# Seven instead of six pairs of each down projection as seven block products, with a second home for the summed weights

## The chip, the cores and the metric

One core of a Trainium2 chip runs the whole program. The metric is the device time of one execution in microseconds (us), the median of repeated runs. The profile is of one execution; its engines are called PE (TensorE, the matmuls), DVE (VectorE), ACT (ScalarE), POOL (GpSimd) and SP (the queue that issues the weight transfers).

## The reference, cut to what matters

A trunk of two layers on 256 positions of width 1024. Each layer adds half a SwiGLU block, a mixer, and half a SwiGLU block again, so there are four SwiGLU blocks, each with an inner width of 2816:

```
def swiglu(x, w_gate, w_up, w_down):
    return (jax.nn.silu(x @ w_gate) * (x @ w_up)) @ w_down

h = h + 0.5 * swiglu(rms_norm(h, ffn1_norm[layer]), ...)
h = h + mixer(rms_norm(h, mix_norm[layer]))
h = h + 0.5 * swiglu(rms_norm(h, ffn2_norm[layer]), ...)
```

The part that matters here is the last product, `(256 x 2816) @ (2816 x 1024)`, called the down projection.

## The kernel before

**Precision.** Every fp32 operand of a product is split in a high part (ACT copies it to fp32r) and a low part (DVE subtracts the high part from it), and a product is three matmuls: high by high, high by low, low by high (`mm3`). So each chunk of weights costs one pass on ACT and one on DVE before PE can use it.

**The stream of weights.** The class `Stream` moves all weights through the core in chunks of 128 x 2048 elements (1 MB), in one order for the whole program. `load_one` fetches a chunk into one of three `raw` buffers; `split_one` makes its parts in one of four `whi`/`wlo` buffers; `pump` does as much of both as the buffers allow, and runs whenever PE's program takes a chunk or gives one back. Instructions are put into each engine's queue at build time; an engine runs its queue in that order and waits where an input isn't ready or a buffer isn't free.

**The down projection.** The 22 tiles of the inner width (128 each) are taken as eleven pairs, named by their first tile, in the order of `DOWN`. The left operand is `hT`, two blocks of 128 positions (t = 0, 1); the right one is two halves of 512 columns (h = 0, 1). For one pair that is a 2 x 2 by 2 x 2 product of blocks: eight block products, 24 matmuls. For the pairs in `MIXED` the kernel computes it with seven block products of sums and differences of blocks, 21 matmuls (`mixed_part`). The sums of the left blocks are made when the inner tile is computed (`mix_rows`: four small DVE operations, one split into `seh`/`sel`). The sums of the weights are made in `split_mixed`: four DVE operations of 128 x 512 into `wx` (one of them changes `raw` in place), then ACT and DVE split `wx` into `wxh` and `wxl` (128 x 1536 each). Of the seven products four need the chunk's own parts (`own`) and three need the sums' parts (`sums`).

**Where the sums' parts lie.** `wxh` and `wxl` have one buffer each. The next mixed pair can write them only when PE has finished the `sums` products of the pair before. To ease that, every second pair does `sums` first and the others `own` first, and `split_mixed` makes its parts in the matching order (`lead`).

**After the products.** `project` ends with the last two pairs of `DOWN` for t = 0 (the residual `x0`, both halves), then for t = 1. The residual adds (`L269`, `L433` and the helper sums `L437`, `L438`), squares (ACT, `L278`), the mean (DVE, `L283`), the root (POOL, `L249`), the scaled copy `xn` (ACT, `L320`), PE's transposes (`L342`) and the split into `xTh`/`xTl` (`L352` on ACT, `L354` on DVE) lead to the first matmuls of the next block (`L381` to `L383`). `xTh`/`xTl` hold the turned x of the current block; the gate and up products (`colwise`, `L391` to `L393`) read them, and nothing reads them during a down projection.

Of the kernel before, what the change touches and what calls it, by code (L numbers as in the profile page):

```python
# [10 lines left out]
F32 = mybir.dt.float32  # L11
# [18 lines left out]
HEAT = 9  # L30
DOWN = [4, 6, 8, 0, 10, 12, 2, 14, 16, 18, 20]
MIXED = (6, 8, 10, 12, 14, 16)

# [5 lines left out]
class Stream:  # L39


    def __init__(self, nc, pools):
        self.nc, (self.raw_pool, self.hi_pool, self.lo_pool) = nc, pools
        self.specs, self.raws, self.parts = [], {}, {}
        self.loaded = self.split = self.done = self.next = self.mixes = 0

    def add(self, src, nk, w, shift=0, pieces=2, mixed=False):
# [48 lines left out]
    def split_mixed(self, j, raw, hi, lo):  # L96
        nc = self.nc
        lead = self.mixes % 2 == 0
        self.mixes += 1
        b11, b12, b21, b22 = (raw[:, i * 512 : (i + 1) * 512] for i in range(4))  # L100
        wx = self.mix_pool.tile([128, 3, 512], F32, name="wx")
        wxh, wxl = (self.mix_pool.tile([128, 3, 512], F32R, name=m) for m in ("wxh", "wxl"))
        nc.vector.tensor_sub(wx[:, 0, :], b22, b12)
        if not lead:
            self.split_piece(hi[:, 1024:], lo[:, 1024:], raw[:, 1024:])
        nc.vector.tensor_sub(b12, b12, b11)
        nc.vector.tensor_add(wx[:, 1, :], wx[:, 0, :], b11)
        nc.vector.tensor_sub(wx[:, 2, :], b21, wx[:, 1, :])  # L108
        if lead:
            self.split_piece(wxh, wxl, wx)  # L110
            self.split_piece(hi[:, 1024:], lo[:, 1024:], raw[:, 1024:])
        self.split_piece(hi[:, :1024], lo[:, :1024], raw[:, :1024])
        if not lead:
            self.split_piece(wxh, wxl, wx)
        self.parts[j] += (wxh, wxl)

    def pump(self):
        n = len(self.specs)
        while True:
            if self.loaded < n and self.loaded - RAW < self.split:  # L120
                self.load_one()
            elif self.split < self.loaded and self.split - SPL < self.done:
                self.split_one()
            else:
                break
# [24 lines left out]
def trunk(ctx: ExitStack, tc: tile.TileContext, a, out):  # L150
# [250 lines left out]
    def project(tiles, order, nfinal, factor, nxt, after=None, mixed={}):  # L401
# [10 lines left out]
        def mixed_part(k, w):  # L412
# [4 lines left out]
            x = [[v[:, j, :] for v in w[2:]] for j in range(3)]  # L417
            own = [((0, 0), a[1][0], b[1][0]), ((0, 1), e[2], b[1][1]), (1, a[0][0], b[0][0]), (5, e[0], b[0][1])]
            sums = [(7, a[0][1], x[0]), (6, e[1], x[1]), ((1, 0), a[1][1], x[2])]
            for key, s, m in sums + own if i % 2 == 0 else own + sums:  # L420
                single = type(key) is int
                if key not in banks:
                    banks[key] = bank()
                first = i == 0 if single else started(*key)
                mm3(banks[key], *s, *m, first, single and i == len(mixed) - 1)
# [232 lines left out]
    def ffn(phase, begin=None):  # L658
        with ExitStack() as pools:
# [55 lines left out]
            def mix_rows(k, hm):  # L715
# [5 lines left out]
                nc.vector.tensor_sub(e[:, 2, :], a12, e[:, 1, :])  # L721
                mixed[k] = [mq.tile([128, 3, 128], F32R, name=f"{n}{k}") for n in ("seh", "sel")]
                split(*mixed[k], e)
# [7 lines left out]
            else:  # L731
# [3 lines left out]
                finish(1)  # L735
            mq = st.mix_pool = pools.enter_context(tc.tile_pool(name="mq", bufs=1))
            mixed = {}
            for k in range(6 if begin else 2, FT, 2):
# [14 lines left out]

            turn_all()
            project(hT, [k + j for k in DOWN for j in range(2)], 4, 0.5, phase + 1, mixed=mixed)

# [319 lines left out]
```

## Time and profile before

| what | value |
|---|---|
| median of 3 runs | 925.23 us (924.93 to 925.3) |
| time of the profiled execution | 924.85 us |
| its span, first to last instruction | 923.1 us |
| PE busy | 915.7 us, 99% |
| DVE busy | 691.9 us, 75% |
| ACT busy | 538.2 us, 58% |

The profiled execution took 1.75 us more than its span, and 0.38 us less than the median. "Busy" is the time in which an engine runs an instruction; the durations of matmuls overlap, so what a matmul costs is read from one start to the next. The four down projections start at 126.92, 395.63, 573.62 and 860.71 us of the span.

### The profile page before, as it was taken

What the parts mean: (1) busy time and instruction counts of PE and PEld (TensorE: products, weight loads), DVE (VectorE), ACT (ScalarE), POOL (GpSimd) and SP (SyncE); (2) the same over time, 40 slices, a digit from 0 to 9 for tenths busy, and PEclk for the clock granted to TensorE, in tenths of its full rate; (3) what the DMA queues carried; (4) which work ended last, traced back from release to release, by engine and by line L of the source; (5) the groups of instructions that cost most, each with busy time, mean ns of one, the idle gap of its engine ahead of it and who ended that gap; (6) DMA issues with size and microseconds to landing.
All of it is one profiled execution on the core that took longest, in us unless ns stands there. A gap on an engine that the chain in (4) does not pass through costs nothing.

```text
span 923.1 us, 15780 instructions
## 1 busy us (share of the span) xinstructions
PE 915.7 (99%) x6442; PEld 843.2 (91%) x6442; DVE 691.9 (75%) x1044; ACT 538.2 (58%) x842; POOL 35.5 (4%) x53
## 2 busy tenths in 40 slices
PE   9999999999999999999999999999999999999997
PEld 8999998889889999988899999888989799999886
DVE  6886779977657566879876678898656575677797
ACT  6754555585867455546664555556756674555552
POOL 0000000000000000000000000000323100000000
PEclk9999999999999999999999999999999999999999
DMA  9885554757526766536486665473744457665351
GB/s 324 270 275 182 186 180 141 270 175 249 167 91 191 221 185 195 192 131 242 153 274 185 195 207 179 162 243 129 250 150 146 129 167 225 203 204 185 137 182 45
DMA packets 125704, 175.79 MB, mean 190 GB/s; under 512 B 3264, under 2 KB 104768, under 8 KB 125632
## 3 DMA queue, kind: packets, MB, share of 16 engines
q1 hardware_dynamic: 123952, 172.60, 57.5%
q10 hardware_dynamic: 1680, 2.19, 0.8%
q8 instruction: 50, 0.82, 0.4%
q14 instruction: 22, 0.18, 0.1%
HBM read 173.73 MB, written 1.05 MB: 189 GB/s over the span
## 4 chain that ended last, share of the span: by engine, by line
PE 99%; issue 1%; DVE 0%; ACT 0%; POOLq 0%; POOL 0%
PE bank L391 18%; PE bank L393 18%; PE bank L392 18%; PE bank L458 5%; PE bank L462 5%; PE bank L459 5%; PE bank L239 4%; PE bank L237 4%; PE bank L238 4%; PE bank L381 3%; PE bank L383 3%; PE bank L382 3%; PE bank L822 1%; PE bank L782 1%; PE bank L342 1%; PE bank L810 1%
## 5 line engine op out<-in xcount | busy, mean ns | idle before, releaser
L93 ACT ACTIVATE whi<-raw 128x1024 fp32r<-128x1024 f32 (+1 forms) x336 | 329.0, 1029 | 238.8 <-PE bank L392 102.8
L94 DVE TENSOR_TENSOR wlo<-raw,whi 128x1024 fp32r<-128x1024 f32 (+1 forms) x336 | 385.1, 1184 | 84.3 <-ACT whi L93 83.7
L391 PE MATMUL bank<-xTh,whi 128*128 128x256 f32 x1440 | 399.7, 278 | 0.0
L393 PE MATMUL bank<-xTh,wlo 128*128 128x256 f32 x1440 | 398.2, 277 | 0.0
L392 PE MATMUL bank<-xTl,whi 128*128 128x256 f32 x1440 | 398.2, 276 | 0.0
L391 PEld LDWEIGHTS bank<-xTh,whi 128*128 128x128 f32 x1440 | 270.3, 188 | 1.3 <-issue 1.2
L392 PEld LDWEIGHTS bank<-xTl,whi 128*128 128x128 f32 x1440 | 270.8, 188 | 0.1
L393 PEld LDWEIGHTS bank<-xTh,wlo 128*128 128x128 f32 x1440 | 270.5, 188 | 0.0
L674 DVE TENSOR_TENSOR hm<-sil,bank 128x512 f32<-128x512 f32 x38 | 26.1, 687 | 57.2 <-PE bank L393 57.1
L458 PE MATMUL bank<-whi,hTh 128*128 128x512 f32 x152 | 59.8, 393 | 0.0
L459 PE MATMUL bank<-wlo,hTh 128*128 128x512 f32 x152 | 59.2, 390 | 0.0
L242 ACT ACTIVATE hTh<-hm 128x512 fp32r<-128x512 f32 x39 | 24.5, 627 | 50.1 <-DVE hm L719 38.9
L462 PE MATMUL bank<-whi,hTl 128*128 128x512 f32 x152 | 51.4, 389 | 0.0
L94 DVE TENSOR_TENSOR wxl<-wx,wxh 128x1536 fp32r<-128x1536 f32 x24 | 42.1, 1755 | 11.3 <-ACT wxh L93 11.2
L381 PE MATMUL bank<-whi,xTh 128*128 128x512 f32 x112 | 44.4, 397 | 0.0
L383 PE MATMUL bank<-whi,xTl 128*128 128x512 f32 x112 | 43.8, 391 | 0.0
L382 PE MATMUL bank<-wlo,xTh 128*128 128x512 f32 x112 | 43.6, 390 | 0.0
L93 ACT ACTIVATE wxh<-wx 128x1536 fp32r<-128x1536 f32 x24 | 35.5, 1481 | 11.6 <-DVE wx L108 7.7
L249 POOL TENSOR_TENSOR rstd<-ms,half_neg 128x1 f32<-128x1 f32 x14 | 8.1, 582 | 797.2 <-DVE ms L283 792.9
L462 PEld LDWEIGHTS bank<-whi,hTl 128*128 128x128 f32 x152 | 28.5, 188 | 6.0
L459 PEld LDWEIGHTS bank<-wlo,hTh 128*128 128x128 f32 x152 | 28.6, 188 | 5.6
L458 PEld LDWEIGHTS bank<-whi,hTh 128*128 128x128 f32 x152 | 28.6, 188 | 5.5
(165 smaller groups left out, 1150.5 us busy)
## 6 DMA issues: line engine op xcount, KB each, us to landing
raw<-in_ffn_w_down SPq DMA_DIRECT2D x44, 1024.0 KB, 5.0
raw<-in_ffn_w_gate SPq DMA_DIRECT2D x38, 1024.0 KB, 5.5
raw<-in_ffn_w_up SPq DMA_DIRECT2D x38, 1024.0 KB, 5.4
raw<-in_c_w_in SPq DMA_DIRECT2D x12, 1024.0 KB, 5.4
raw<-in_ab_w_in SPq DMA_DIRECT2D x10, 1024.0 KB, 5.4
raw<-in_ffn_w_up SPq DMA_DIRECT2D x12, 512.0 KB, 6.5
raw<-in_ffn_w_gate SPq DMA_DIRECT2D x8, 512.0 KB, 4.0
raw<-in_ab_w_out SPq DMA_DIRECT2D x4, 1024.0 KB, 5.0
```

What stands on the lines that cost most here:

```text
L93: self.nc.scalar.activation(hi, raw, AF.Copy)
L94: self.nc.vector.tensor_sub(lo, raw, hi.bitcast(F32))
L237: nc.tensor.matmul(p, sh, mh, start=start, stop=False)
L381: nc.tensor.matmul(p, xh, w[0][:, k, :], start=k0 + k == 0, stop=False)
L382: nc.tensor.matmul(p, xh, w[1][:, k, :], start=False, stop=False)
L383: nc.tensor.matmul(p, xl, w[0][:, k, :], start=False, stop=k0 + k == KD - 1)
L391: nc.tensor.matmul(p, h, xh, start=k == 0, stop=False)
L392: nc.tensor.matmul(p, h, xl, start=False, stop=False)
L393: nc.tensor.matmul(p, l, xh, start=False, stop=k == KD - 1)
L458: nc.tensor.matmul(banks[t, h], sh, w[0][:, kw, cs], start=first, stop=False)
L459: nc.tensor.matmul(banks[t, h], sh, w[1][:, kw, cs], start=False, stop=False)
L462: nc.tensor.matmul(banks[t, h], sl, w[0][:, kw, cs], start=False, stop=last)
```

## The change

- `MIXED` gains pair 18, and `DOWN` changes: mixed pair 6 first, plain pair 4 in the tail instead of pair 18.
- All mixed pairs do `own` first and `sums` last, and `split_mixed` makes the parts of `raw`'s second half first, then its first half, and the sums' parts last.
- The sums' parts have two homes in turn: `near` (`wxh`/`wxl` as before) for pairs 6, 10, 14, 18, and `far` for pairs 8, 12, 16: the buffers of `xTh`/`xTl`.
- `held` keeps `pump` from splitting a pair bound for `far` until the down projection begins, since the turned x is still read there until then.
- The left sums' parts of pair 6 lie in a buffer of `xn`, the scratch of the norm.

```
-DOWN = [4, 6, 8, 0, 10, 12, 2, 14, 16, 18, 20]
-MIXED = (6, 8, 10, 12, 14, 16)
+DOWN = [6, 0, 8, 10, 12, 2, 14, 16, 18, 4, 20]
+MIXED = (6, 8, 10, 12, 14, 16, 18)
...
     def split_mixed(self, j, raw, hi, lo):
...
-        wxh, wxl = (self.mix_pool.tile([128, 3, 512], F32R, name=m) for m in ("wxh", "wxl"))
+        wxh, wxl = self.mix_tiles[self.mixes % 2]()
+        self.mixes += 1
         nc.vector.tensor_sub(wx[:, 0, :], b22, b12)
-        if not lead:
-            self.split_piece(hi[:, 1024:], lo[:, 1024:], raw[:, 1024:])
+        self.split_piece(hi[:, 1024:], lo[:, 1024:], raw[:, 1024:])
         nc.vector.tensor_sub(b12, b12, b11)
         nc.vector.tensor_add(wx[:, 1, :], wx[:, 0, :], b11)
         nc.vector.tensor_sub(wx[:, 2, :], b21, wx[:, 1, :])
...
         self.split_piece(hi[:, :1024], lo[:, :1024], raw[:, :1024])
-        if not lead:
-            self.split_piece(wxh, wxl, wx)
+        self.split_piece(wxh, wxl, wx)
         self.parts[j] += (wxh, wxl)
+
+    def held(self):
+        return not self.specs[self.split][-1] and self.mixes % 2 and not self.open
...
-            elif self.split < self.loaded and self.split - SPL < self.done:
+            elif self.split < self.loaded and self.split - SPL < self.done and not self.held():
...
-            for key, s, m in sums + own if i % 2 == 0 else own + sums:
+            for key, s, m in (((0, 0), a[1][0], b[1][0]), ((0, 1), e[2], b[1][1]), (1, a[0][0], b[0][0]),
+                              (5, e[0], b[0][1]), (7, a[0][1], x[0]), (6, e[1], x[1]), ((1, 0), a[1][1], x[2])):
...
+                if k == MIXED[0]:
+                    both = wk.tile([128, D], F32, name="xn").bitcast(F32R)
+                    mixed[k] = [both[:, c : c + 384].rearrange("p (j c) -> p j c", j=3) for c in (0, 384)]
...
+            def near():
+                return [mq.tile([128, 3, 512], F32R, name=n) for n in ("wxh", "wxl")]
+
+            def far():
+                return [xp.tile([128, KD, NT, 128], F32R, name=n).rearrange("p k t c -> p (k t c)")[:, :1536]
+                        .rearrange("p (j c) -> p j c", j=3) for n in ("xTh", "xTl")]
+
+            st.mix_tiles = near, far
...
             turn_all()
+            st.open = True
             project(hT, [k + j for k in DOWN for j in range(2)], 4, 0.5, phase + 1, mixed=mixed)
```

The lines of the kernel shift: `L94` becomes `L95`, `L106` to `L108` become `L105` to `L107`, `L269` becomes `L267`, `L342` becomes `L340`, `L237` to `L239` become `L235` to `L237`.

**DVE at the end of the second down projection, before** (`wlo` is a chunk's low part, `wxl` the low part of the sums, `wx` and `raw` the four sums, the last row the first residual add):

```order
L94 TENSOR_TENSOR wxl<-wx,wxh 128x1536
L94 TENSOR_TENSOR wlo<-raw,whi 128x1024
L103 TENSOR_TENSOR wx<-raw 128x512
L106 TENSOR_TENSOR raw<-raw 128x512
L107 TENSOR_TENSOR wx<-wx,raw 128x512
L108 TENSOR_TENSOR wx<-raw,wx 128x512
L94 TENSOR_TENSOR wlo<-raw,whi 128x1024 x2
L94 TENSOR_TENSOR wxl<-wx,wxh 128x1536
L94 TENSOR_TENSOR wlo<-raw,whi 128x1024 x3
L433 SCALAR_TENSOR_TENSOR x_81<-bank,x_81 128x512
```

The same place after the change; `xTl` here is the far home of the sums of pair 16, and the sums after it are those of pair 18:

```order
L95 TENSOR_TENSOR wlo<-raw,whi 128x1024 x2
L95 TENSOR_TENSOR xTl<-wx,xTh 128x1536
L95 TENSOR_TENSOR wlo<-raw,whi 128x1024
L103 TENSOR_TENSOR wx<-raw 128x512
L105 TENSOR_TENSOR raw<-raw 128x512
L106 TENSOR_TENSOR wx<-wx,raw 128x512
L107 TENSOR_TENSOR wx<-raw,wx 128x512
L95 TENSOR_TENSOR wlo<-raw,whi 128x1024 x2
L95 TENSOR_TENSOR wxl<-wx,wxh 128x1536
L95 TENSOR_TENSOR wlo<-raw,whi 128x1024 x3
L430 SCALAR_TENSOR_TENSOR x_81<-bank,x_81 128x512
```

The last mixed pair is now the seventh, and from its `wxl` to the residual adds the same work follows as before.

**PE at the end of the same projection, before**: the transposes of the scaled copy of x0, and the first matmuls of the next block behind them:

```order
L342 MATMUL bank<-ident,xn 128x128 x4
L458 MATMUL bank<-whi,hTh 128x512
L459 MATMUL bank<-wlo,hTh 128x512
L462 MATMUL bank<-whi,hTl 128x512
L342 MATMUL bank<-ident,xn 128x128 x4
L458 MATMUL bank<-whi,hTh 128x512
L459 MATMUL bank<-wlo,hTh 128x512
L462 MATMUL bank<-whi,hTl 128x512
L381 MATMUL bank<-whi,xTh 128x512
```

The same place after the change:

```order
L455 MATMUL bank<-whi,hTh 128x512
L340 MATMUL bank<-ident,xn 128x128 x4
L456 MATMUL bank<-wlo,hTh 128x512
L340 MATMUL bank<-ident,xn 128x128 x4
L459 MATMUL bank<-whi,hTl 128x512
L379 MATMUL bank<-whi,xTh 128x512
```

The transposes stand four matmuls later in PE's queue: 46 matmuls after the last mixed pair instead of 42, and two projection matmuls instead of six lie between them and the next block.

## Rows read from the trace of the kernel before

**Rows 1.** The page: busy time by engine, and the chain that ended last.

```profile
PE 915.7 (99%) x6442; PEld 843.2 (91%) x6442; DVE 691.9 (75%) x1044; ACT 538.2 (58%) x842; POOL 35.5 (4%) x53
...
PE 99%; issue 1%; DVE 0%; ACT 0%; POOLq 0%; POOL 0%
```

**Rows 2.** Four down projections up to the tail: window, length, each engine's busy time.

```profile
126.92:171.80 44.88, 44.88 (x201) 37.17 (x200) 40.75 (x43) 25.90 (x27) 0.00 (x0) 1.00 0.56 189
395.63:440.54 44.91, 44.91 (x201) 37.18 (x199) 40.12 (x41) 25.85 (x25) 0.00 (x0) 1.00 0.56 188
...
sum 179.61, PE 179.61 PEld 148.71 DVE 160.55 ACT 102.02 POOL 0.00; mean PE 44.90 PEld 37.18 DVE 40.14 ACT 25.51 POOL 0.00
```

**Rows 3.** Timeline of PE, second projection: start, length, line, operation.

```profile
395.63 0.40 PE L458 MATMUL bank<-whi,hTh 128*128 128x512 f32 x1
...
440.54 0.39 PE L458 MATMUL bank<-whi,hTh 128*128 128x512 f32 x1
...
450.06 0.60 PE L342 MATMUL bank<-ident,xn 128*128 128x128 f32 x4
...
452.33 0.40 PE L381 MATMUL bank<-whi,xTh 128*128 128x512 f32 x1
```

**Rows 4.** Groups by line and shape, whole span: count, busy us, mean ns of one.

```profile
L94 DVE TENSOR_TENSOR wlo<-raw,whi 128x1024 fp32r<-128x1024 f32 x312 | 369.7, 1222 | 81.6 <-ACT whi L93 81.0
L93 ACT ACTIVATE whi<-raw 128x1024 fp32r<-128x1024 f32 x312 | 315.6, 1058 | 235.0 <-PE bank L392 102.8 <-issue 38.4 <-DVE raw L106 32.3
...
L94 DVE TENSOR_TENSOR wxl<-wx,wxh 128x1536 fp32r<-128x1536 f32 x24 | 42.1, 1755 | 11.3 <-ACT wxh L93 11.2
L93 ACT ACTIVATE wxh<-wx 128x1536 fp32r<-128x1536 f32 x24 | 35.5, 1481 | 11.6 <-DVE wx L108 7.7 <-PE bank L239 3.9
...
L718 DVE TENSOR_TENSOR sil<-hm 128x128 f32<-128x128 f32 x24 | 7.0, 292 | 0.8
```

**Rows 5.** Timeline of DVE in the second projection: one mixed pair without a pause.

```profile
413.79 1.75 DVE L94 TENSOR_TENSOR wxl<-wx,wxh 128x1536 fp32r<-128x1536 f32 x1
415.58 0.69 DVE L103 TENSOR_TENSOR wx<-raw 128x512 f32<-128x512 f32 x1
416.30 0.69 DVE L106 TENSOR_TENSOR raw<-raw 128x512 f32<-128x512 f32 x1
416.91 0.69 DVE L107 TENSOR_TENSOR wx<-wx,raw 128x512 f32<-128x512 f32 x1
417.63 0.69 DVE L108 TENSOR_TENSOR wx<-raw,wx 128x512 f32<-128x512 f32 x1
418.24 2.35 DVE L94 TENSOR_TENSOR wlo<-raw,whi 128x1024 fp32r<-128x1024 f32 x2
420.51 1.75 DVE L94 TENSOR_TENSOR wxl<-wx,wxh 128x1536 fp32r<-128x1536 f32 x1
```

**Rows 6.** The same timeline where DVE was idle: [idle us before, releaser].

```profile
395.90 0.69 DVE L674 TENSOR_TENSOR hm<-sil,bank 128x512 f32<-128x512 f32 x1 [0.53 <-PE bank L393]
396.82 2.36 DVE L94 TENSOR_TENSOR wlo<-raw,whi 128x1024 fp32r<-128x1024 f32 x2 [0.23 <-ACT whi L93]
...
402.44 1.23 DVE L94 TENSOR_TENSOR wlo<-raw,whi 128x1024 fp32r<-128x1024 f32 x1 [2.66 <-ACT whi L93]
404.92 1.76 DVE L94 TENSOR_TENSOR wxl<-wx,wxh 128x1536 fp32r<-128x1536 f32 x1 [1.25 <-ACT wxh L93]
```

**Rows 7.** Timelines of DVE and ACT: last mixed pair to the scaled copy.

```profile
436.13 1.76 DVE L94 TENSOR_TENSOR wxl<-wx,wxh 128x1536 fp32r<-128x1536 f32 x1
...
446.67 0.69 DVE L269 SCALAR_TENSOR_TENSOR x<-bank,x 128x512 f32<-128x512 f32 x1
448.15 0.21 DVE L283 TENSOR_SCALAR ms<-ss 128x1 f32<-128x1 f32 x1 [0.79 <-ACT xn L278]
449.09 1.34 ACT L320 ACTIVATE xn<-x,rstd 128x512 f32<-128x512 f32 x2 [0.97 <-POOL rstd L249]
```

**Rows 8.** Instructions on the tile raw, 380 to 450 us: transfer times.

```profile
DMA to landing us min/median/max: 3.9/5.2/8.1
```

More of the change, by code (lines that the diff above doesn't have):

```diff
@@ L45, in __init__ @@
         self.loaded = self.split = self.done = self.next = self.mixes = 0
+        self.open = False
     def add(self, src, nk, w, shift=0, pieces=2, mixed=False):
@@ L97, in split_mixed @@
         nc = self.nc
-        lead = self.mixes % 2 == 0
-        self.mixes += 1
         b11, b12, b21, b22 = (raw[:, i * 512 : (i + 1) * 512] for i in range(4))
         wx = self.mix_pool.tile([128, 3, 512], F32, name="wx")
-        wxh, wxl = (self.mix_pool.tile([128, 3, 512], F32R, name=m) for m in ("wxh", "wxl"))
+        wxh, wxl = self.mix_tiles[self.mixes % 2]()
+        self.mixes += 1
         nc.vector.tensor_sub(wx[:, 0, :], b22, b12)
-        if not lead:
-            self.split_piece(hi[:, 1024:], lo[:, 1024:], raw[:, 1024:])
+        self.split_piece(hi[:, 1024:], lo[:, 1024:], raw[:, 1024:])
         nc.vector.tensor_sub(b12, b12, b11)
@@ L108, in split_mixed @@
         nc.vector.tensor_sub(wx[:, 2, :], b21, wx[:, 1, :])
-        if lead:
-            self.split_piece(wxh, wxl, wx)
-            self.split_piece(hi[:, 1024:], lo[:, 1024:], raw[:, 1024:])
         self.split_piece(hi[:, :1024], lo[:, :1024], raw[:, :1024])
-        if not lead:
-            self.split_piece(wxh, wxl, wx)
+        self.split_piece(wxh, wxl, wx)
         self.parts[j] += (wxh, wxl)
+    def held(self):
+        return not self.specs[self.split][-1] and self.mixes % 2 and not self.open
     def pump(self):
@@ L417, in mixed_part @@
             x = [[v[:, j, :] for v in w[2:]] for j in range(3)]
-            own = [((0, 0), a[1][0], b[1][0]), ((0, 1), e[2], b[1][1]), (1, a[0][0], b[0][0]), (5, e[0], b[0][1])]
-            sums = [(7, a[0][1], x[0]), (6, e[1], x[1]), ((1, 0), a[1][1], x[2])]
-            for key, s, m in sums + own if i % 2 == 0 else own + sums:
+            for key, s, m in (((0, 0), a[1][0], b[1][0]), ((0, 1), e[2], b[1][1]), (1, a[0][0], b[0][0]),
+                              (5, e[0], b[0][1]), (7, a[0][1], x[0]), (6, e[1], x[1]), ((1, 0), a[1][1], x[2])):
                 single = type(key) is int
@@ L721, in mix_rows @@
                 nc.vector.tensor_sub(e[:, 2, :], a12, e[:, 1, :])
-                mixed[k] = [mq.tile([128, 3, 128], F32R, name=f"{n}{k}") for n in ("seh", "sel")]
+                if k == MIXED[0]:
+                    both = wk.tile([128, D], F32, name="xn").bitcast(F32R)
+                    mixed[k] = [both[:, c : c + 384].rearrange("p (j c) -> p j c", j=3) for c in (0, 384)]
+                else:
+                    mixed[k] = [mq.tile([128, 3, 128], F32R, name=f"{n}{k}") for n in ("seh", "sel")]
                 split(*mixed[k], e)
@@ L736, in ffn @@
             mq = st.mix_pool = pools.enter_context(tc.tile_pool(name="mq", bufs=1))
+            st.mixes, st.open = 0, False
+            def near():
[4 more added lines that the diff above has]
+            st.mix_tiles = near, far
             mixed = {}
```

## The prediction

> **What bounds the kernel now.** I read the page first: PE is busy for 915.7 of 923.1 us and makes 99% of the chain that ended last [rows 1], so only fewer matmuls, or a wait that PE doesn't have yet, can move the time. DVE's 75% looks like a quarter in reserve, but that is an average over the whole span, so next I read the stage that changes, by windows. In the four down projections up to the tail PE has no gap (44.90 us busy on average, the length of the windows), and DVE is busy for 40.14 of them [rows 2]. Its reserve there is 4.8 us, not a quarter. Third, I read where that reserve lies. In the second projection it is nearly all at the front: DVE idles 0.53, 0.23, 2.66 and 1.25 us before four instructions up to 404.92, 4.67 us in sum [rows 6]; from there on it runs one instruction after another [rows 5] until the squares of x0. Last, I read the end of the stage: the second residual add to x0 starts at 446.67, the mean at 448.15, the scaled copy at 449.09 [rows 7], and PE transposes the copy at 450.06 [rows 3]. The copy's first half is done at 449.09 + 1.34/2 = 449.76, so PE comes for it about 0.3 us after it is there. That chain is the next to bind after PE itself.
>
> **What is removed.** One block product of three matmuls per projection. A 128x512 matmul costs what lies between starts: from 440.54 to 450.06 there are 42, so 0.2267 us each [rows 3]. Three are 0.68 us; four projections 2.72 us. Nothing but waits can take this back. The TensorE page of the Trainium skill ("TensorE: Matmul & The Clock Gate", the part on the 2.5 ns floor) has 215.7 ns from start to start for this size at 2.4 GHz; by it the gain would be an estimated 2.59 us; the trace has the duration, so it is used.
>
> **What is added.** On DVE, per projection, the four sums of one more pair and their low part. The sums take 415.58 to 418.24, 2.66 us, the low part about 1.7 more [rows 5]: 4.4 us. On ACT one more pass of 1.48 us [rows 4] over the sums; ACT is busy for 25.5 us of 44.9 [rows 2], so it is covered, and costs only where DVE waits for it. Earlier, while the gate and up products run, pair 18 also gets its left sums: four operations of 0.29 us [rows 4] and a split. PE needs them only 39 us later; the reserve of that stage hides them (over the whole span DVE is idle a quarter of the time), and I cost them at nothing. The second home needs no copy. It takes away the wait of one pair's sums for PE's reading of the pair before, which is behind the 1.25 us and part of the 2.66 us in [rows 6]. The scratch of the norm as home for pair 6 costs nothing: its products come first in the projection, and the norm needs the buffer some 50 us later.
>
> **The added wait.** `held` lets pair 8's sums be split only after the last up product. Behind it in ACT's queue stand the first splits of pairs 10 and 12. I set time 0 at the first matmul of the second projection, 395.63 [rows 3]. ACT splits pair 10's first half at about 0.1, then the last inner tile, then pair 8's sums (1.48 us) until 3.1; DVE follows with their low part until 4.8. PE wants it at 4.76 + 5.44 + 2.72 = 12.9 (21 matmuls of pair 6, 24 of pair 0, 12 of pair 8). Hidden, with 8 us to spare.
>
> **The balance on DVE.** From 4.8 on DVE's queue up to the low part of pair 18's sums holds fourteen low parts of half a chunk (418.24 to 420.51 for two: 1.135 each [rows 5]), 15.9 us; five sets of sums, two of them interleaved with low parts so that no operation waits for the one right before it, 13.1; four low parts of sums at 1.7 and the last at 1.76, 8.6. It can't run without any pause: pairs 10 and 12 have their sums' high part (1.48 us on ACT after the last of the four sums) covered only by one low part of 1.135, which leaves about 0.5 us each time with the handover, and one low part waits about 0.1 us for a transfer that is issued when its buffer comes free and lands 5.2 us later [rows 8]. Together 4.8 + 15.9 + 13.1 + 8.6 + 1.1 = 43.5, and pair 18's last ordinary low part is done one step earlier, at 41.75.
>
> PE starts pair 18 at six mixed pairs and two plain ones, 6 x 4.76 + 2 x 5.44 = 39.44, and wants that ordinary part eight matmuls later, at 41.25: **a wait of 0.5**. Seven matmuls after that it wants the sums' part: 41.75 + 1.59 = 43.34 against 43.5, 0.1 more. So about 0.6 of the 0.68 us is given back before the tail. Before, the last pair's sums' part was started at 436.13 and done 1.76 later, at 42.26 from time 0 [rows 7], and PE took it at 43.1, eight matmuls before the end of the stage (44.91 - 8 x 0.2267).
>
> **The norm chain.** From the start of the last sums' low part to the second add to x0 there lie 10.54 us before (436.13 to 446.67 [rows 7]), and the same work stands there now. It starts at 41.7, so the add comes at 52.2; up to 0.9 later if the copy that the helper sums wait for stands on ACT behind a split whose transfer lands late. Before it was at 51.04. From the add to the copy at PE there were 3.1 to 3.4 us, so the transposes can start at 55.4 to 56.4. PE arrives at 44.20 + 0.6 + 46 x 0.2267 = 55.2: **a wait of 0.2 to 1.2**. Behind the transposes four matmuls fewer stand than before, so the next block's first matmul comes 2.27 - 0.91 = 1.36 us after them (450.06 to 452.33 [rows 3]): at 56.8 to 57.8, against 56.70 before. The half for t = 1 hangs on the same DVE queue, where its adds come as late; for that I allow 0 to 0.6 more. A transition thus costs 0.1 to 1.7 us net, and I take the middle, 0.95. There are three: the fourth projection ends the program, has no next chunks to split, and keeps 0.68 - 0.6 = 0.1 of gain.
>
> **Sum.** 3 x 0.95 - 0.1 = 2.75. On the profiled execution's 924.85 us (0.38 us under the median) that is 927.6, and **928.0** against the median of 925.23.
>
> **The rule against the change.** The trace first: DVE is busy for 40.14 us of the 44.90 of a projection [rows 2], and 4.4 us go on it while PE's part shrinks to 44.2. The Trainium skill, "Perfetto Trace Analysis", section Identifying the Most-Contended Engine, has occupancy as a fair measure of the limit for VectorE but not for TensorE, and says that the most contended engine can change over a kernel's regimes. By that rule alone VectorE would limit the stage at 40.14 + 4.4 = 44.5 us, and 0.4 us of each projection would stay gained; the page says nothing on chains, so this is the second rival below.
>
> **Rivals.** (1) *All is hidden*: the 4.67 us of idle time at the front [rows 6] take the 4.4 us, and the double home lets DVE run ahead. Then the time is 925.23 - 2.72 = 922.5. For it speaks that the two numbers match; against it that 1.1 us of pauses come back inside the stage and 0.8 at its front, and that PE's margin was 0.8 us at the last pair and 0.3 at the transposes. It decides in my favour as soon as DVE reaches the second add over 0.3 us later than now. (2) *DVE limits the projections, but the norm doesn't wait*: 0.4 us of each projection stays: 925.23 - 1.6 = 923.6, up to 925.5 if one of the waits exists. (3) *A transfer comes late*: three raw buffers are refilled only when DVE is done with one; landings go up to 8.1 us [rows 8], and one such in a stage without reserve is 2.9 us on DVE. One in each of two projections: 925.23 + 2.75 + 2 x 2.9 = 933.8.
>
> **Chances.** Forecast 0.55, its own range 925.5 (transitions at their low end) to 930.1 (all near the high one); rival 1 0.22, 2 0.15, 3 0.08. About 0.2%, 1.85 us, is what a measurement of this kernel can tell from no change. Faster than 923.4: rival 1 and a little of 2, 0.24. Within: most of 2 and the lower part of the forecast, 0.30. Slower than 927.1: the rest, 0.46. For 8 in 10 the range goes down to rival 1 and up to the end of the forecast: 922.3 to 930.6.
>
> **What would show it.** PE with gaps, where it has none now: before the ordinary low part of pair 18 (waiting for DVE's `wlo`) and before the transposes (waiting for ACT's `xn`) in the first three projections; DVE above 97% busy from 5 to 45 us of each projection; the second add to x0 at 52.2 or later from the projection's start, against 51.04. I am wrong if DVE reaches the low part of pair 18's sums before 42.5, if PE's row shows no wait behind the start, or if the projections' windows are 0.6 us shorter each.

## The result, and the profile after

| | before | changed |
|---|---|---|
| median | 925.14 us (924.83 to 925.35, 6 runs) | 931.71 us (931.06 to 932.62, 6 runs) |
| ratio | | 1.0072 (95% interval 1.0059 to 1.0085) |
| span of the profiled execution | 923.1 us | 930.9 us |

The change makes the kernel 6.57 us slower. The forecast was 928.0, with a range up to 930.6: the direction was right, the size less than half.

The page of the changed kernel, the lines that answer to [rows 1]:

```profile
PE 918.0 (99%) x6430; PEld 839.6 (90%) x6430; DVE 715.6 (77%) x1084; ACT 545.1 (59%) x850; POOL 35.4 (4%) x53
PE 76%; DVE 14%; DMA 3%; ACT 3%; issue 3%; POOL 0%; ACTq 0%; SPq 0%; POOLq 0%; DVEq 0%
```

PE runs the twelve matmuls fewer and is still "99% busy"; DVE went from 75 to 77%. Neither line shows what happened. The second does: the chain that ended last ran over PE for 99% of the span before, and now leaves it for a quarter of the span, 14% of it on DVE. The busy shares by stage, in windows of the same lengths as [rows 2] (from the start of each projection: window, length, busy time of PE, PEld, DVE, ACT, POOL):

```profile
127.37:172.25 44.88, 44.87 (x198) 36.49 (x197) 43.29 (x47) 27.37 (x27) 0.00 (x0) 1.00 0.51 169
398.05:442.96 44.91, 44.65 (x197) 36.45 (x196) 43.05 (x45) 27.20 (x25) 0.00 (x0) 1.00 0.52 174
577.49:622.40 44.91, 44.19 (x194) 35.82 (x193) 42.52 (x44) 26.89 (x27) 0.00 (x0) 1.00 0.49 170
866.48:911.39 44.91, 43.69 (x192) 35.30 (x191) 41.99 (x44) 25.22 (x23) 0.00 (x0) 1.00 0.42 140
sum 179.61, PE 177.41 PEld 144.06 DVE 170.85 ACT 106.68 POOL 0.00; mean PE 44.35 PEld 36.02 DVE 42.71 ACT 26.67 POOL 0.00
```

DVE is at 42.71 of 44.90 us where it was at 40.14, and PE, which had no gap in these windows, now loses up to 1.2 us in one. The waits of PE by line and releaser (us in total, times, longest):

```profile
PE bank L340 <- ACT xn L318: 2.1, 3, 0.9
PE bank L236 <- DVE wlo L95: 1.7, 3, 0.7
PE bank L534 <- DVE warm L226: 1.1, 1, 1.1
PE bank L235 <- ACT whi L94: 0.5, 1, 0.5
PE bank L379 <- ACT xTh L350: 0.4, 1, 0.4
```

Only the wait for `warm`, at the program's start, was there before. The first two are the two that the prediction named: pair 18's ordinary low part, and the transposes that need the scaled copy of x0. In the second projection, on PE (the first answers to the first of [rows 3], the last two to its last two), and on DVE (answering to [rows 7]; the first row holds the first half of pair 20 and then the half of pair 18 that is split last, the first half of its `raw`, as the order of the queue has it):

```profile
398.05 0.40 PE L235 MATMUL bank<-whi,hTh 128*128 128x512 f32 x1
...
439.85 0.50 PE L236 MATMUL bank<-wlo,hTh 128*128 128x512 f32 x1 [0.26 <-DVE wlo L95]
...
454.46 0.66 PE L340 MATMUL bank<-ident,xn 128*128 128x128 f32 x4 [0.87 <-ACT xn L318]
...
455.86 0.39 PE L379 MATMUL bank<-whi,xTh 128*128 128x512 f32 x1
```

```profile
437.44 2.35 DVE L95 TENSOR_TENSOR wlo<-raw,whi 128x1024 fp32r<-128x1024 f32 x2
439.71 1.75 DVE L95 TENSOR_TENSOR wxl<-wx,wxh 128x1536 fp32r<-128x1536 f32 x1
...
451.26 0.69 DVE L267 SCALAR_TENSOR_TENSOR x<-bank,x 128x512 f32<-128x512 f32 x1
452.75 0.21 DVE L281 TENSOR_SCALAR ms<-ss 128x1 f32<-128x1 f32 x1 [0.79 <-ACT xn L276]
```

Counted from 398.05: pair 18's last ordinary low part is done at 41.74 (437.44 + 2.35; forecast 41.75), its sums' part at 43.41 (forecast 43.5), the second add to x0 starts at 53.21 (forecast 52.2, up to 53.1), the transposes at 56.41 (forecast 55.4 to 56.4), the next block at 57.81 (forecast 56.8 to 57.8). The mechanism stood: DVE was on the forecast at pair 18, and the norm behind it came at the late end of its bounds or just past it.

Where the 7.8 us of the two spans lie, from PE's first matmul of each projection to the first of the next, in us:

| from the projection's start | before | changed | more | forecast |
|---|---|---|---|---|
| first to second projection | 268.71 | 270.68 | 1.97 | 0.95 |
| second to third | 177.99 | 179.44 | 1.45 | 0.95 |
| third to fourth | 287.09 | 288.99 | 1.90 | 0.95 |
| fourth to the last matmul | 55.82 | 57.17 | 1.35 | -0.1 |
| last matmul to the end of the span | 6.57 | 7.25 | 0.68 | 0 |

The remaining 0.45 us lie ahead of the first projection, in the loading at the start, where the two kernels do the same work; that start lay up to 1.1 us apart in the profiles of the kernels below, and the median of the runs has less of it (6.57 against 7.8).

### The profile page after: what moved, and what is told of

It reads as the page before. It is cut to its first block, busy times and chain, and to the rows that moved or that the text cites. A ratio compares the mean times of both kernels' runs of the same rounds, so it can differ in the third digit from the quotient of the medians.

```text
span 930.9 us, 15792 instructions
## 1 busy us (share of the span) xinstructions
PE 918.0 (99%) x6430; PEld 839.6 (90%) x6430; DVE 715.6 (77%) x1084; ACT 545.1 (59%) x850; POOL 35.4 (4%) x53
## 4 chain that ended last, share of the span: by engine, by line
PE 76%; DVE 14%; DMA 3%; ACT 3%; issue 3%; POOL 0%; ACTq 0%; SPq 0%; POOLq 0%; DVEq 0%
PE bank L389 18%; PE bank L391 18%; PE bank L390 18%; DVE wlo L95 6%; PE bank L379 3%; PE bank L380 3%; PE bank L381 3%; PE bank L455 2%; DMA raw<-in_ffn_w_down 2%; PE bank L459 2%; PE bank L456 2%; DVE wx L103 1%; DVE raw L105 1%; PE bank L340 1%; PE bank L834 1%
## 5 line engine op out<-in xcount | busy, mean ns | idle before, releaser
L94 ACT ACTIVATE whi<-raw 128x1024 fp32r<-128x1024 f32 (+1 forms) x336 | 330.7, 1030 | 255.1 <-PE bank L390 112.8
L95 DVE TENSOR_TENSOR wlo<-raw,whi 128x1024 fp32r<-128x1024 f32 (+1 forms) x336 | 386.5, 1184 | 78.3 <-ACT whi L94 77.7
L456 PE MATMUL bank<-wlo,hTh 128*128 128x512 f32 x120 | 47.0, 391 | 0.0
L455 PE MATMUL bank<-whi,hTh 128*128 128x512 f32 x120 | 46.8, 390 | 0.0
L459 PE MATMUL bank<-whi,hTl 128*128 128x512 f32 x120 | 41.7, 391 | 0.0
L241 DVE TENSOR_TENSOR hTl<-hm,hTh 128x512 fp32r<-128x512 f32 x39 | 26.9, 689 | 5.8 <-ACT hTh L240 5.8
L352 DVE SCALAR_TENSOR_TENSOR xTl<-bank,gT,xTh 128x128 fp32r<-128x128 f32 x80 | 23.1, 345 | 9.5 <-ACT xTh L350 9.5
L95 DVE TENSOR_TENSOR wxl<-wx,wxh 128x1536 fp32r<-128x1536 f32 x16 | 28.1, 1754 | 1.9 <-ACT wxh L94 1.9
L350 ACT ACTIVATE xTh<-bank,gT 128x128 fp32r<-128x128 f32 x80 | 23.3, 372 | 8.6 <-PE bank L340 5.5
L236 PE MATMUL bank<-wlo,hTh 128*128 128x512 f32 (+1 forms) x68 | 26.1, 384 | 1.7 <-DVE wlo L95 1.7
```

The lines of the kernel that those rows point to most:

```text
L94: self.nc.scalar.activation(hi, raw, AF.Copy)
L95: self.nc.vector.tensor_sub(lo, raw, hi.bitcast(F32))
L241: nc.vector.tensor_sub(lo, src, hi.bitcast(F32))
L455: nc.tensor.matmul(banks[t, h], sh, w[0][:, kw, cs], start=first, stop=False)
L456: nc.tensor.matmul(banks[t, h], sh, w[1][:, kw, cs], start=False, stop=False)
L459: nc.tensor.matmul(banks[t, h], sl, w[0][:, kw, cs], start=False, stop=last)
```

## The experiments

Each was run four times or more beside the kernel before. In the first expectations "Theory A" is that DVE's added work is the price, B that a transfer held in the queues is, C that the moves themselves are; later ones say what their letters stand for. Where an expectation speaks of pair 18's "second half", it is the half that is split last, the first half of its `raw`. The ratios are to the kernel before, and code is cut to the lines that matter.

**Six pairs, all the moves kept.**

```
-MIXED = (6, 8, 10, 12, 14, 16, 18)
+MIXED = (6, 8, 10, 12, 14, 16)
```

> Pair 18 is taken out of the seven again; the new order, the second home of the sums' parts, the hold of pair 8 and the borrowed scratch of pair 6 stay. Theory A (DVE has no reserve: its 4.4 us of added work per projection make pair 18 and the norm late): the 4.4 us are gone, no wait of PE is left, and three matmuls per projection are back, so 924.5 to 926. Theory B (a late transfer: the first half of the last pair stands in the queues ahead of the previous pair's second half and waits for its own transfer there): part of the waits stays, 926 to 928. Theory C (the moves themselves cost, not the seventh pair): 929 or more.

925.54 us, 1.0004 (0.9996 to 1.0013), and no wait of PE but the one for `warm`. The order, the second home, the hold and the borrowed scratch cost nothing that can be measured. C falls: the price belongs to pair 18.

**All of pair 18's extra work taken off DVE and ACT**, PE's program unchanged:

```
+        if self.mixes == len(MIXED) - 1:
+            self.mixes += 1
+            self.split_piece(hi[:, 1024:], lo[:, 1024:], raw[:, 1024:])
+            self.split_piece(hi[:, :1024], lo[:, :1024], raw[:, :1024])
+            self.parts[j] += tuple(t[:, :1536].rearrange("p (j c) -> p j c", j=3) for t in (hi, lo))
+            return
```

> The changed kernel with none of pair 18's extra work on DVE and ACT: its sums and the two parts of them are not made, and PE multiplies 1536 columns of the chunk's own parts in their place, so the output is not the reference's. PE's instructions are the changed kernel's. Theory A (the extra 4.4 us on DVE are the whole price): no wait is left and the twelve matmuls are gained, 925.54 - 2.72 = 922.8, at most 923.6. Rival E (with three matmuls fewer, the norm chain can't follow whatever DVE has to do, so the gain can't show): 924.5 to 925.5.

923.25 us, 0.9979 (0.9970 to 0.9988). The chain that ended last is PE's again, and the four projections show no gap:

```profile
PE 98%; DMA 1%; issue 1%; SPq 0%; ACT 0%; DVE 0%; POOLq 0%; POOL 0%
```

```profile
sum 179.61, PE 179.61 PEld 148.40 DVE 164.37 ACT 102.31 POOL 0.00; mean PE 44.90 PEld 37.10 DVE 41.09 ACT 25.58 POOL 0.00
```

This is the run that settles the main point. The matmuls are worth about what the sum had for them: 2.29 us between the medians of this run and the six pairs, 2.72 by the working. And making pair 18's sums and their parts, 4.4 us on DVE and 1.5 on ACT per projection, costs 931.71 - 923.25 = 8.46 us with all that hangs on it. One thing that hangs on it is a transfer: in the second projection pair 20's is issued 30.1 us after the start here, where the changed kernel has 32.9 (the rows stand below, with the four operations left out), so the 8.46 us are not the instructions' time alone. DVE's mean is 41.09 in these windows, only 1.6 under the changed kernel's, though 4.4 us of work are gone: part of what fills the windows is work on the next stage's chunks, which DVE here reaches earlier.

**All of that work kept, PE's saving undone.** Pair 18 is multiplied as a plain pair:

```
-            project(hT, [k + j for k in DOWN for j in range(2)], 4, 0.5, phase + 1, mixed=mixed)
+            project(hT, [k + j for k in DOWN for j in range(2)], 4, 0.5, phase + 1,
+                    mixed={k: v for k, v in mixed.items() if k != 18})
```

> The changed kernel with all of its work on DVE and ACT, but PE multiplies pair 18 as a plain pair: 24 matmuls for 21, its sums' parts are made and not read, and its right half is the changed one, so the output is not the reference's. Theory A: DVE sets the time, so the three matmuls that PE does more per projection (0.68 us) cost little: 930 to 932.5, about the changed kernel's. Theory P (PE sets the time and the waits are small extras): 931.7 + 2.7 = 934.4. Theory C (the price lies in the seventh pair's products and their order on PE): 925 to 927.

930.48 us, 1.0057 (1.0044 to 1.0069). Twelve matmuls more on PE, 2.72 us, and the time is 1.2 us less, not more. So in these stages PE's matmuls are not what sets the time. One thing helps this run beside that: its last mixed pair on PE is 16, so the adds to x0 can begin a pair earlier.

**The last pair's split moved behind pair 18's sums.** On ACT and DVE the first half of pair 20 stands ahead of the last half of pair 18, and waits there for its own transfer:

```
+                if self.mixes == len(MIXED) and self.split in self.behind:
+                    high, low = self.sums
+                    with tc_of[0].issue_after(high.ins), tc_of[0].issue_after(low.ins):
+                        self.split_one()
```

Here `behind` holds pair 20's chunk, and `high`, `low` are the split of pair 18's sums.

> The changed kernel with one thing moved: the split of the last pair of each projection (20) is queued behind the split of pair 18's sums on ACT and DVE, so its transfer can't hold pair 18's second half. No work is added or taken away. Theory A: only what DVE idled for that transfer comes back, about 0.5 us in the third projection and 1.1 us in the fourth (its gaps there of 0.53 and 1.06 us); the waits before the transposes stay: 930 to 930.8. Theory B: all waits at pair 18 go, 0.4, 0.5, 1.2 and 1.9 us over the four projections: about 927.7. Theory C: 931.7, no change.

928.95 us, 1.0041 (1.0027 to 1.0054): 2.8 us back for an order of issue alone, more than A said and less than B. From projection to projection it is 1.48, 1.26 and 0.98 us over the kernel before, and the last one's matmuls end at 55.83, as before (55.82). So the place of that split is a part of the price, largest in the fourth projection. What the rest is this run doesn't tell.

**Four of DVE's operations left out** (the sums of pair 18, 2.66 us per projection).

```
-        nc.vector.tensor_sub(wx[:, 0, :], b22, b12)
+        sums = self.mixes < len(MIXED)
+        if sums:
+            nc.vector.tensor_sub(wx[:, 0, :], b22, b12)
+        else:
+            wx = raw[:, :1536].rearrange("p (j c) -> p j c", j=3)
...
-        nc.vector.tensor_sub(b12, b12, b11)
-        nc.vector.tensor_add(wx[:, 1, :], wx[:, 0, :], b11)
-        nc.vector.tensor_sub(wx[:, 2, :], b21, wx[:, 1, :])
+        if sums:
+            nc.vector.tensor_sub(b12, b12, b11)
+            nc.vector.tensor_add(wx[:, 1, :], wx[:, 0, :], b11)
+            nc.vector.tensor_sub(wx[:, 2, :], b21, wx[:, 1, :])
```

> The changed kernel without the four sums of pair 18 on DVE (2.66 us per projection): the sums' parts are split from the untouched chunk instead, so the output is not the reference's. PE, ACT and the transfers do what they did. Theory A: DVE reaches everything behind them 2.66 us earlier, more than any wait of PE that was seen (0.4 to 1.9 us), so nearly all of the matmuls' gain shows: 922.4 to 924. Theory B: the transfer of the last pair is issued and lands at the same time as before, so DVE only waits longer in front of it: 929 to 931. Theory C: 930 to 931.7.

928.60 us, 1.0034 (1.0022 to 1.0047). Not A's 922.4 to 924. In the second projection (from 396.31) DVE is done with pair 18 at 39.5 us, where the changed kernel has 43.41, and then it and ACT stand before the last pair's split:

```profile
437.52 2.36 DVE L95 TENSOR_TENSOR wlo<-raw,whi 128x1024 fp32r<-128x1024 f32 x2 [1.72 <-ACT whi L94]
```

```profile
436.43 2.02 ACT L94 ACTIVATE whi<-raw 128x1024 fp32r<-128x1024 f32 x2 [3.21 <-DMA raw<-in_ffn_w_down]
```

A good part of the time given to DVE goes into waiting for the transfer, and the transfer itself moved. Pair 20's issue in the second projection, in the changed kernel, in this run, and in the one without any parts:

```profile
430.95 0.37 SPq L66 DMA_DIRECT2D raw<-in_ffn_w_down  x1
```

```profile
431.36 0.37 SPq L66 DMA_DIRECT2D raw<-in_ffn_w_down  x1
```

```profile
425.81 0.37 SPq L66 DMA_DIRECT2D raw<-in_ffn_w_down  x1
```

That is 32.9, 35.05 and 30.1 us after the projection's start, with landings at 37.9, 40.1 and 35.1. With the sums left out, two more low parts of half a chunk stand ahead of pair 16's last one in DVE's queue, so its buffer comes free 2.1 us later; with no parts made at all, pair 18's own buffer is done with at 30.1, and the transfer is issued then. So the expectation's "PE, ACT and the transfers do what they did" did not hold. This run and the one without any parts are 5.4 us apart, and differ by a low part on DVE, a high part on ACT and 5 us in that transfer: the runs don't tell these apart.

**The same with pair 20's split moved behind.**

> The changed kernel with the last pair's split behind pair 18's sums, and without pair 18's four sums on DVE (2.66 us per projection; the sums' parts are split from the untouched chunk, so the output is not the reference's). In the run without the sums alone DVE idled 1.7 us for the last pair's transfer, and 0.6 more, and so reached the second add to x0 only 1.4 us earlier. Theory A (DVE's queue is the bound; what the moves gave came back in the next stage because the work itself stayed): now the relief reaches the add, no wait of PE over 0.3 us is left, 922.4 to 924. Theory B (transfers hold the path whatever DVE has to do): 927 to 928.6.

928.44 us, 1.0035 (1.0021 to 1.0048). My theory missed again, by 4 us. PE's waits at pair 18 are gone, but the transfer is issued as late as in the run before (35.1 us), DVE still idles 1.65 us for it, and the second add to x0 starts about 51.8 us after the projection's start (448.0 - 396.24), against 53.21 in the changed kernel, 51.04 before, and 50.20 in the run without parts. With three matmuls fewer PE comes 0.68 earlier than before, so it waits 3.3 us in sum before the three transitions' transposes.

**The next stage's second chunk queued behind the norm of x0**, alone, with pair 20's move, with both the move and the four operations left out, and with the move and without any parts:

```
+        if st.limit:
+            st.limit = None
+            behind(n0.squared, mean, st.pump)
...
+            if phase < 5:
+                st.limit = st.next + len(DOWN) + 1
```

> The changed kernel with one thing moved: the split of the next stage's second chunk, in the first three projections, is queued behind the mean of x0's norm on DVE and behind the second square on ACT. Pair 18 and the last pair stay as they are. Theory A: transposes wait because four low parts of next chunks (4.5 us on DVE, and on ACT a high part that waits up to 3.1 us for its transfer) stand ahead of the second add to x0; without the second chunk's two the add comes 2.4 us earlier and the waits before the transposes (0.7, 1.0, 0.8 us, and 0.3 to 1.2 in the block after them) go: 928.2 to 929.5. Rival D: the wait only moves to the next block, whose second chunk is now split late: 931 to 933.

> The last pair's split behind pair 18's sums and the next stage's second chunk behind the norm of x0, together. Theory A: both waits are separate, so the gains add: 928.95 less 0.7 to 1.2 per transition, 925.3 to 926.8, and what is left is the wait of 0.6 us per projection for the low part of pair 18's sums, which eats the matmuls' 0.68. Rival D: 929 or more.

> The run with relief (last pair's split behind pair 18's sums, pair 18's four sums left out on DVE, so the output is not the reference's), and the next stage's second chunk queued behind the norm of x0 as well. With the relief alone DVE stood idle for 2.2 us behind transfers between pair 18 and the second add to x0, had four low parts of next chunks (4.6 us) ahead of that add, and PE still waited 1.1 us at the transposes. Theory A (DVE's queue: both its length and its order make the norm late): with two of the four behind the add, the add comes 2.3 us earlier, the transposes don't wait, and since DVE has room now, the next block doesn't either: 922.4 to 924. Rival D (whatever is moved, the next block waits instead, as in the run that moved only this): 927.5 to 929.

> As the run before, and with the two moves: the last pair's split behind pair 18's, the next stage's second chunk behind the norm of x0. Theory A: no more than the run before, 922.4 to 923.6. Rival E: the norm's queue was what held it, so this run is faster than the one before by 1 us or more.

931.17 us (1.0065, 1.0053 to 1.0078), 929.89 (1.0048, 1.0035 to 1.0062), 926.99 (1.0019, 1.0010 to 1.0027) and 925.48 (1.0005, 0.9996 to 1.0014). Alone it takes the wait from the transposes (54.7 us after the projection's start, not 56.4, in the second) and gives most of it back behind them. Beside pair 20's move the median is 0.9 us higher (the intervals overlap). Where DVE has nothing extra to do, both moves together lose 2.2 us (925.48 against 923.25), 0.65 to 0.74 per transition, all of it behind the first matmul of the next block: the two low parts then stand between the adds to x1 and the turned x, and PE waits for the turned x. In the run with pair 20's move alone beside it, from PE's waits:

```profile
PE bank L391 <- DVE xTl L362: 1.2, 3, 0.5
```

In the first two Rival D holds, and the fourth met neither of its theories: this order moves the lateness, and doesn't remove it. Only with the four operations left out does it help (926.99 against 928.44, between the two theories).

**Where in the program: seven pairs in the fourth projection alone**, without and with pair 20's move.

```
+    mixes = [MIXED[:6], MIXED[:6], MIXED[:6], MIXED]
```

> Seven pairs in the fourth projection alone, six in the other three; all else as in the changed kernel. With six in all four the run gave 925.54. Theory A: the fourth projection pays by itself, 1.2 us for the waits up to the end of its matmuls and about 0.7 behind them: 926.8 to 927.5. If the price came from what earlier projections leave behind: 924.9 to 925.5 (a gain of up to 0.68).

> Seven pairs in the fourth projection alone, with the last pair's split behind pair 18's sums there; nothing is left out. The fourth projection has no next chunks to split. Theory A: it ends at best as with six pairs, since DVE's last low part of the sums still comes 0.5 us late and the adds behind it lag: 925.2 to 926. If the transfer was all that held it: 924.6 to 925 (0.68 gained on 925.54).

926.0 us (1.0009, 1.0000 to 1.0018) and 925.88 (1.0007, 0.9998 to 1.0015), against 925.54 with six pairs: 0.3 to 0.5 us more, which the intervals don't tell from no change. The changed kernel loses 2.03 us in the same stage, with the same work there. The first expectation met neither of its theories; the second is A's. What differs in the rows is the last transfer. From the chain that ended last, in the changed kernel:

```profile
899.47 6.43 DMA raw<-in_ffn_w_down
905.90 0.02 issue
905.92 0.04 ACTq L94
905.96 0.04 issue
906.00 1.07 ACT whi L94
907.08 0.02 issue
907.10 2.36 DVE wlo L95 x2
909.46 1.71 DVE wxl L95
911.18 1.14 DVE wlo L95
912.32 0.61 DVE x L430
```

and on ACT and DVE with seven pairs in the fourth projection alone:

```profile
899.17 2.02 ACT L94 ACTIVATE whi<-raw 128x1024 fp32r<-128x1024 f32 x2 [2.94 <-DMA raw<-in_ffn_w_down]
```

```profile
900.83 2.35 DVE L95 TENSOR_TENSOR wlo<-raw,whi 128x1024 fp32r<-128x1024 f32 x2
```

Both transfers are issued 32.9 to 33.0 us after the projection's start (899.47 - 866.48; 894.35 - 861.45), when DVE is done with pair 16's buffer. One takes 6.43 us and DVE idles 1.06 for it, the other is there after 4.7 and DVE doesn't idle. From the projection's start to the end of the span it is 64.4 us in the changed kernel, 62.6 with seven pairs here alone, and 62.5 with six: some 1.8 of the 2.03 us go with that transfer. Even so the seventh pair gains nothing here: its parts are still late (PE waits 0.3 us for one), and the adds behind them, which at the end of the program nothing covers, with it.

Why the transfer takes longer at the same place no run tried, but the traces show what stands beside it. In the changed kernel one packet of 16 KB of the instruction queue falls into it (DMA queues from 899.47 to 905.90 us: packets, MB, share):

```profile
q8 instruction: 1, 0.02, 1.7%
```

Take pair 20's transfer in the third and in the fourth projection of all 18 profiles. In 20 of these 36 such a packet starts 1.0 to 2.7 us after the issue, and they took 5.35 to 6.43 us; in the other 16 it doesn't, and they took 4.72 to 5.04. No run moved the packet, so that it is the cause is not shown.

**The second home undone.**

```
-        wxh, wxl = self.mix_tiles[self.mixes % 2]()
+        wxh, wxl = self.mix_tiles[0]()
...
-        return not self.specs[self.split][-1] and self.mixes % 2 and not self.open
+        return not self.specs[self.split][-1] and False
```

> The second home undone: all seven pairs put their sums' parts in the one pair of tiles, and pair 8 isn't held back. All else as in the changed kernel. Each pair's sums' parts must then wait until PE has read the pair before. Theory A: DVE, without reserve, loses about the 0.5 to 1 us per pair that ACT waits there: 934 to 940. If the second home and the hold cost more than they give: 929 to 931.

952.3 us, 1.0291 (1.0277 to 1.0305), far above the 934 to 940 expected. With seven pairs in this order the second home, with its hold, is worth 20 us. Without it ACT's pass over the sums waits, in the second projection, 1.02 us for PE before one pair and 2.53 us before the next (for that the profile names no releaser), and PE waits 13.7 us in sum before the three transitions' transposes.

**DVE's work given to POOL**: the sums of pairs 10 and 12; the low part of pair 4; the latter with pair 20's move and the chunk behind the norm.

```
+        e = nc.gpsimd if self.mixes in (3, 4) else nc.vector
```

```
+                                 nc.gpsimd if j in self.pooled else nc.vector)
```

> The changed kernel with the sums of pairs 10 and 12 (eight operations of 128x512) on POOL in place of DVE. DVE loses 5.3 us of work per projection early in it. From POOL's 1.06 us for 128x256 and 0.68 us for 128x128 in the kernel before I work out 1.8 us for each, 14.7 us for the eight, which start about when the projection starts; PE wants pair 12's sums at 22.4 us. Theory A: DVE runs ahead and all waits go: 922.5 to 924; if POOL takes twice as long, or slows DVE, 926 or more. Theory B: the gain is small, since the transfer decides: 929 to 931.

> The changed kernel with the low part of pair 4 (two halves of 128x1024 per projection, 2.3 us on DVE) on POOL, where 128x512 took 1.3 to 2.2 us in the run with sums on POOL, so 5 to 9 us for the two; PE wants them about 10 us after they can start. Theory A: DVE reaches pair 18's last low parts 2.3 us earlier, the waits there (0.4, 0.5, 1.2, 1.9) go but for what the last pair's transfer holds, and the norm comes earlier: 927 to 929. Theory B (transfers alone): POOL gives pair 4's buffer back some 5 us later, the next stage's transfer with it: 932 or more.

> All three together: last pair behind pair 18's sums, next stage's second chunk behind the norm of x0, pair 4's low part on POOL. Theory A: no wait at pair 18 is left, none at the transposes; the time is that before less the twelve matmuls, plus at most 0.3 us per transition: 922.4 to 923.6, faster than both kernels. Rival: POOL is too late for pair 4 or slows DVE on a shared path: 925 or more.

959.56 us (1.0375, 1.0360 to 1.0389), 938.13 (1.0143, 1.0129 to 1.0157) and 940.27 (1.0164, 1.0150 to 1.0178), all far above what Theory A had. For the first, `wx` has one buffer, so POOL can't start pair 12's sums before DVE has split pair 10's, and 6.9 us of POOL per pair come into the path. For the other two, see the last section: POOL's work and DVE's hold each other up.

## Why the prediction was wrong

- **The added wait (pair 8 held), the second home, the borrowed scratch at nothing**: right, by the run with six pairs.
- **The matmuls' 2.72 us**: about right; 2.3 to 2.6 of it came out where nothing else stood in the way (2.29 by the medians; 0.69, 0.68, 0.58 and 0.68 less per stage than with six pairs, by PE's starts).
- **The balance on DVE**: the step "pair 18's last ordinary low part at 41.75, its sums' part at 43.5" was met to 0.1 us in the second projection (41.74, 43.41). Its term "one low part waits about 0.1 us for a transfer that lands 5.2 us later" was mis-sized: DVE idled 0.53 us there in the third projection and 1.06 in the fourth (transfers of 5.89 and 6.43 us), and what stands behind it in the queue is pair 18's last half. So PE lost 0.5 and 0.6 us at pair 18 in the first two projections, by its starts over the matmuls' own spacing, as the working had it (0.6), but 1.2 and 1.9 in the third and fourth.
- **The norm chain**: the chain was right, and its terms were too small. The working gave 0.1 to 1.7 us per transition, 0 to 0.6 of it for t = 1, and took 0.95 (the middle is 0.9). Measured were 1.97, 1.45 and 1.90. The next block began 0.74, 1.11 and 1.57 us later than before, where the working had 0.1 to 1.1, and another 1.23, 0.34 and 0.33 us came behind its first matmul, where it had up to 0.6. In the second projection DVE had pair 18's sums done on the forecast and lost 1.0 us between them and the second add, 0.84 of it idle: for a bank of PE's, and for a copy on ACT that stood behind a split waiting for its transfer, as the working's "up to 0.9 later" has it:

```profile
445.93 0.69 DVE L267 SCALAR_TENSOR_TENSOR x<-bank,x 128x512 f32<-128x512 f32 x1 [0.46 <-PE bank L459]
447.00 0.69 DVE L434 TENSOR_TENSOR wx<-bank,wx 128x512 f32<-128x512 f32 x1 [0.38 <-ACT wx L433]
```

```profile
445.44 1.06 ACT L94 ACTIVATE whi<-raw 128x1024 fp32r<-128x1024 f32 x1 [3.06 <-DMA raw<-in_ffn_w_up]
```

  Taking the middle treats the late ends as independent. That they come together, because all these steps stand in one queue of DVE, is a reading that fits the three transitions; no run tests it by itself.
- **"The fourth projection ... keeps 0.1 of gain"**: this step failed outright; it lost 2.03. I let the price end with PE's last wait and left out that the end of the program hangs on DVE's adds, and I had the last transfer at 5.2 us where it took 6.43. The chain that ended last leaves DVE, from 893.86 to the root of the norm at 920.57, only for that transfer and two passes on ACT.
- **The rivals**: the first (all hidden) and the second fell. The second counted DVE's busy time, as the Trainium skill has it ("Perfetto Trace Analysis", Identifying the Most-Contended Engine: occupancy is a fair measure for VectorE). Here 42.71 of 44.9 us busy went with a loss of 1.5 to 2 us per stage, and 41.09 with none: occupancy named the engine whose work was the price, and told nothing of its size. The working's remark that the page says nothing on chains is wrong: it has a section, Identifying Dependency Chains, on the semaphores that an instruction waits for, but no price for them. The third rival (a late transfer, 0.08) was a part of what happened: not 2.9 us twice by chance, but 0.5 to 1.1 on top of the full queue.

What is shown: the price comes with pair 18's preparation on DVE and ACT, not with the moves (925.54 with six pairs), and not with PE's part (without the preparation 923.25; with it and PE's saving undone 930.48). And 2.8 us of it hang on the order of one split. What stays open is how the price divides between the time of the instructions on DVE, the pass on ACT, and the buffers and transfers that move with them. Leaving out 60% of the work on DVE gave back 3.1 to 3.3 of 8.46 us, but issued the last pair's transfer 2.1 us later; leaving out all of it issued that transfer 2.8 us earlier. No run holds the transfer in place while DVE's work changes. No version with the seventh pair that computes the reference's output was faster than the kernel before; the best of them with seven pairs in all four projections was 928.95.

## What to carry to other kernels

When work moves from the bounding engine to a second one, don't compare the second one's free time with the added work: take its queue in order, and ask at each place where the bounding engine waits for it. Where it is full, a late end is likely to meet the next one, so look at the sum of the late ends of the bounds, not only at their middles, and count the end of the program too. A split that waits for its transfer at the head of an in-order queue holds work that is needed earlier; look for that first, since moving it adds no work (2.8 us gained here). And when an experiment leaves work out, read from its trace whether the order of the queues and the transfers stayed as they were, before the difference is put down to the work.

## What was not expected of the hardware

POOL's work and DVE's held each other up. With pair 4's low part on POOL, in the second projection, on POOL (both halves, then the second by itself) and on DVE:

```profile
432.24 6.48 POOL L98 TENSOR_TENSOR wlo<-raw,whi 128x1024 fp32r<-128x1024 f32 x2 [150.81 <-ACT whi L97]
```

```profile
434.80 3.92 POOL L98 TENSOR_TENSOR wlo<-raw,whi 128x1024 fp32r<-128x1024 f32 x1
```

```profile
433.57 2.89 DVE L98 TENSOR_TENSOR xTl<-wx,xTh 128x1536 fp32r<-128x1536 f32 x1 [0.99 <-ACT xTh L97]
436.49 2.78 DVE L106 TENSOR_TENSOR wx<-raw 128x512 f32<-128x512 f32 x1
439.31 0.69 DVE L108 TENSOR_TENSOR raw<-raw 128x512 f32<-128x512 f32 x1
```

While POOL ran (432.24 to 438.72) a low part of sums took DVE 2.89 us in place of 1.75, and a sum 2.78 in place of 0.69; right after, a sum took 0.69 again. DVE lost 3.2 us there and was spared 2.3. The Trainium skill says of this ("GPSIMD Engine Reference", Specifications) that the two share their interfaces to SBUF and contend for DVE instructions with two inputs there; both of these have two, and the trace agrees.

The rows look like turns, not like a lower speed. DVE's low part ends 1.6 us after POOL's first half, about its own time; POOL's second half ends 2.26 us after DVE's low part; DVE's sum ends 0.55 us after POOL's second half. It is the same with the sums of pairs 10 and 12 on POOL: a DVE low part that begins 0.2 us before POOL's sum takes its usual 1.23 us, the sum takes 2.18 in place of 1.29, and DVE's next low part then 2.32 in place of 1.22:

```profile
422.64 1.29 POOL L107 TENSOR_TENSOR wx<-wx,raw 128x512 f32<-128x512 f32 x1
424.01 2.18 POOL L108 TENSOR_TENSOR wx<-raw,wx 128x512 f32<-128x512 f32 x1
```

```profile
423.81 3.46 DVE L95 TENSOR_TENSOR wlo<-raw,whi 128x1024 fp32r<-128x1024 f32 x2 [3.64 <-ACT whi L94]
```

In these rows whichever begins first keeps its time, and the other takes longer by about what is left of it. No run tries other kinds of instructions.
